# A one-core decoder trunk: the first value unit split in halves, a square moved, the last tile read by column halves, and other schedule offsets

## The chip, the cores and the metric

The kernel runs on one core of one Trainium2 chip. The metric is the device time of one execution in microseconds (us). Times here are from three timed runs of the kernel before and from one profiled execution of it.

## The reference

One decoder block over 512 tokens of 1024 channels, in float32: a mixer of three branches, a merge, and a convolutional feed-forward net.

```python
h = rmsnorm(x); proj = h @ w_in                      # 1024 -> 9216
y_a = (gb * conv3(gc * v)) @ w_a_out                 # short gated convolution
y_b = silu(layernorm(conv31(u * sigmoid(ug)))) @ w_b_out
k, vm = split(rmsnorm(mem) @ w_kv)                   # 256 memory tokens, 4 heads
y_c = softmax(q k^T / 16) vm @ w_att_out
x = x + (sigmoid(g0)*y_a + sigmoid(g1)*y_b + sigmoid(g2)*y_c) @ w_o
u = conv3(rmsnorm(x) @ w_up)                         # 1024 -> 2 * 2816
x = x + (silu(gt) * up) @ w_down
out = rmsnorm(x)
```

## The kernel before, in words

**Products.** TensorE multiplies in float32r. Each operand is split in a high part (ScalarE's cast, `whi` for weights) and a low part (VectorE's subtraction of the high part from the value, `wlo`), and each product is three: high by high, high by low, low by high. A *unit* is a weight tile of 128 x 1024, loaded by one DMA of 512 KB (`wf`, six buffers); its `whi` (L444) and `wlo` (L448) live in a ring of four, so a unit's cast waits until TensorE is through with the unit four places earlier. The large products run in Strassen's manner: a *quad* of four weight blocks u, v, s, r takes seven products, forms 1 to 7, instead of eight (`quad_loads`). The forms 5, 6, 7 and 3 need sums of blocks. These are made mostly by adding DMAs issued on POOL (L582: s5, s6, s7, s3), each of which waits until the low part of the form made before it from the same tile is done. The reads r1 to r7 (`quad_reads`, L651 r1, L655 r5, L658, L666 r6, L672 r4, L401) carry the products' banks into tiles; form 6 goes into the bank that r1 has read.

**Order.** Each step is a *job* with an engine, a cost in us, the jobs that it waits for, and the places (rings of tiles, banks of PSUM) that it takes and uses (`Jobs`). TensorE's jobs have a written order. For all others a list schedule picks, again and again, the job that can start earliest by the planner's costs, and of those with the same start the one due first; a job's due time is counted back from the TensorE product that wants it. `LATER` moves the due times of a kind of job, `AHEAD` keeps a kind from starting more than so many us before its due time. The planner adds 0.2, 0.14 and 0.12 us behind a job of TensorE, ScalarE and VectorE. Every engine then runs its instructions in the order in which the schedule emitted them, SP and POOL among them; a job may emit instructions for an engine other than its own (the final scaling is a VectorE job that also emits a ScalarE copy and the two output DMAs, one on ScalarE's queue).

**The start.** Nine products of the identity (L1697) run while the first loads land. The first unit of the keys, K0, is loaded, cast (L818) and subtracted (L822) in halves of 512 columns, and its products (L871) stand as two jobs; the other units come whole: V(0,0), V(0,1), K(1,0), then the second half of the memory tokens, and so on. The values' products are L395 (high by high), L396 and L397 of `product`. The memory tile's square (`msq`, L734) feeds sums of squares (L750), which TensorE takes after five units.

**The up products.** Their quads are `("up", 0)` to `("up", 10)`; weights beyond the third quad are loaded ahead into free large tiles. The reads need the job `temps`, which opens a new tile pool once the normed rows are transposed. Between w_o and the first forms the normed rows are transposed into banks, of which ScalarE makes high parts (L1598) and plain copies (L1611) and VectorE low parts (L1604).

**The end.** The down product has seven forms a to g, each with two banks, one for each tile t of 128 tokens of a half. The last form, g, does for its units 3 to 5 first t = 0 and then t = 1 (`("pd", "g", "rest")`, 15 products of 512 columns). VectorE adds the bank to the row in `x1` (`read`, L1977; the job `rd`), ScalarE squares the row's half with a sum (L1982, `sq` for the right half, `sr` for the left), VectorE adjusts the right half's sum and multiplies by the gain (`hd`, L1988, L1991), ScalarE takes the root (`rt`, L1996), and `sc` inverts it (L2002), scales both halves (L2003 on ScalarE, L2004 on VectorE) and stores them (L2008).

## Time and profile before

| | us |
|---|---|
| timed, median of 3 (lowest to highest) | 931.41 (930.99 to 931.84) |
| the profiled execution | 931.52 |
| its span, first to last instruction | 929.3 |
| busy: TensorE / VectorE / ScalarE | 916.8 / 837.3 / 672.5 |

A row of the instructions in order of time has the start, the length, the engine (PE is TensorE, PEld its weight load, DVE VectorE, ACT ScalarE, a q behind a name that engine's DMA queue), the line of the kernel, the operation, the output and its inputs, the shape, and in brackets how long the engine had been idle and what ended that. A row of the waits has who waited for whom, and then the total in us, how many times, and the longest. A row of stretches has the stretch, its length, then the busy time of PE, PEld, DVE, ACT and POOL with the number of instructions, TensorE's granted clock, the DMA engines' busy share and GB/s. A row of the DMA view has the transfer, the issuing queue, the count, the size of one and the median time from issue to landing.

### The profile page before, as it was taken

The page shows a single profiled execution, that of the slowest core. Times are in us where ns is not written, and L with a number is a line of the kernel's source. Part 1 is how long each engine was busy: PE and PEld are TensorE (multiplying, and loading weights), DVE is VectorE, ACT ScalarE, POOL GpSimd, SP SyncE. Part 2 cuts the span into 40 slices and gives each one's busy share as a digit, 9 for nine tenths or more (in the row PEclk, how much of TensorE's full clock was granted, in tenths as well). Part 3 has the DMA queues.
Part 4 walks back from the last instruction along what each step waited for, and adds up shares of the span by engine and source line. Part 5 has one row for each costly group of instructions (what it writes and reads, how often), then busy time and mean ns, then how long its engine had stood idle before and what let it go on. Part 6 is the DMA issues. An engine that isn't in the chain of part 4 may idle for free.

```text
span 929.3 us, 16689 instructions
## 1 busy us (share of the span) xinstructions
PE 916.8 (99%) x6644; PEld 860.5 (93%) x6644; DVE 837.3 (90%) x948; ACT 672.5 (72%) x908; POOL 126.5 (14%) x153
## 2 busy tenths in 40 slices
PE   8999999999999999999999999999999999999996
PEld 7999999999989999999899888898999999988885
DVE  6898999969889999999996778897899889999986
ACT  7676988759978879878856743766767676765655
POOL 0121111101111112110100011021211121002300
PEclk9999999999999999999999999999999999999998
DMA  9999678857676799967955598499999878779962
GB/s 356 371 269 236 137 171 178 201 133 136 170 185 170 177 191 243 210 174 183 226 115 158 186 314 179 97 246 295 258 226 235 209 141 166 195 268 329 251 125 91
DMA packets 54077, 190.59 MB, mean 205 GB/s; under 512 B 6128, under 2 KB 6256, under 8 KB 54000
## 3 DMA queue, kind: packets, MB, share of 16 engines
q0 software_dynamic: 20880, 75.24, 45.5%
q1 hardware_dynamic: 32400, 113.23, 34.0%
q8 instruction: 52, 0.85, 0.4%
q10 hardware_dynamic: 720, 1.06, 0.3%
q14 instruction: 25, 0.20, 0.1%
HBM read 185.31 MB, written 4.19 MB: 204 GB/s over the span
## 4 chain that ended last, share of the span: by engine, by line
PE 93%; DMA 3%; ACT 2%; DVE 1%; issue 1%; SPq 0%; ACTq 0%; POOLq 0%
PE bank L624 56%; PE bank L395 6%; PE bank L397 6%; PE bank L396 6%; PE bank L1349 5%; PE bank L1350 5%; PE bank L1351 5%; DMA wf<-in_w_up 2%; PE bank L871 2%; DMA mem<-in_mem_t 1%; ACT whi L444 0%; DVE wlo L448 0%; PE ss L750 0%; PE bank L1098 0%; ACT j L1982 0%
## 5 line engine op out<-in xcount | busy, mean ns | idle before, releaser
L444 ACT CAST whi<-wf 128x1024 fp32r<-128x1024 f32 (+1 forms) x195 | 202.9, 1044 | 100.9 <-PE bank L624 40.1
L448 DVE TENSOR_TENSOR wlo<-wf,whi 128x1024 fp32r<-128x1024 f32 (+1 forms) x189 | 228.3, 1214 | 29.8 <-ACT whi L444 29.4
L1170 ACT ACTIVATE tp<-u,pk 128x510 f32<-128x510 f32 (+22 forms) x184 | 119.7, 706 | 7.5 <-DVE acc L1177 6.5
L1177 DVE TENSOR_TENSOR acc<-acc,tp 128x1022 f32<-128x1022 f32 (+22 forms) x92 | 109.5, 1193 | 4.2 <-ACT tp L1170 2.4
L582 POOL DMA_DIRECT2D wf<-in_w_in x48 | 42.5, 894 | 229.7 <-DVE wlo L448 164.0
L624 PE MATMUL bank<-ft6h,wlo 128*128 128x256 f32 x232 | 64.4, 278 | 1.2 <-DVE wlo L448 1.2
L624 PE MATMUL bank<-ft6h,whi 128*128 128x256 f32 x232 | 64.6, 278 | 1.0 <-ACT gt L651 1.0
L624 PE MATMUL bank<-fb10h,whi 128*128 128x256 f32 x232 | 64.4, 278 | 0.0
L624 PE MATMUL bank<-fb00h,whi 128*128 128x256 f32 x232 | 64.4, 278 | 0.0
L624 PE MATMUL bank<-fb00l,whi 128*128 128x256 f32 x232 | 64.3, 277 | 0.0
L624 PE MATMUL bank<-fb00h,wlo 128*128 128x256 f32 x232 | 64.3, 277 | 0.0
L624 PE MATMUL bank<-ft7h,whi 128*128 128x256 f32 x232 | 64.3, 277 | 0.0
L624 PE MATMUL bank<-ft7l,whi 128*128 128x256 f32 x232 | 64.3, 277 | 0.0
L624 PE MATMUL bank<-ft7h,wlo 128*128 128x256 f32 x232 | 64.3, 277 | 0.0
L624 PE MATMUL bank<-fb11h,whi 128*128 128x256 f32 x232 | 64.3, 277 | 0.0
L624 PE MATMUL bank<-ft5h,wlo 128*128 128x256 f32 x232 | 64.2, 277 | 0.0
L624 PE MATMUL bank<-ft5h,whi 128*128 128x256 f32 x232 | 64.2, 277 | 0.0
L624 PE MATMUL bank<-ft5l,whi 128*128 128x256 f32 x232 | 64.2, 277 | 0.0
L624 PE MATMUL bank<-ft6l,whi 128*128 128x256 f32 x232 | 64.2, 277 | 0.0
L624 PE MATMUL bank<-fb10h,wlo 128*128 128x256 f32 x232 | 64.2, 277 | 0.0
L624 PE MATMUL bank<-fb10l,whi 128*128 128x256 f32 x232 | 64.2, 277 | 0.0
L624 PE MATMUL bank<-fb11l,whi 128*128 128x256 f32 x232 | 64.1, 276 | 0.0
(392 smaller groups left out, 3143.8 us busy)
## 6 DMA issues: line engine op xcount, KB each, us to landing
wf<-in_w_in SPq DMA_DIRECT2D x52, 512.0 KB, 4.9
wf<-in_w_in POOLq DMA_DIRECT2D x48, 512.0 KB, 5.8
wf<-in_w_up SPq DMA_DIRECT2D x29, 512.0 KB, 5.3
wf<-in_w_up POOLq DMA_DIRECT2D x28, 512.0 KB, 6.9
wf<-in_w_down SPq DMA_DIRECT2D x15, 512.0 KB, 4.2
wf<-in_w_v SPq DMA_DIRECT2D x8, 512.0 KB, 10.1
wf<-in_w_att_out SPq DMA_DIRECT2D x8, 512.0 KB, 3.9
wf<-in_w_a_out SPq DMA_DIRECT2D x8, 512.0 KB, 3.8
```

The lines of the kernel that those rows point to most:

```text
L395: nc.tensor.matmul(ps, s_hi, w_hi, start=start, stop=False, skip_group_check=again)
L396: nc.tensor.matmul(ps, s_hi, w_lo, start=False, stop=False, skip_group_check=again)
L397: nc.tensor.matmul(ps, s_lo, w_hi, start=False, stop=stop, skip_group_check=again)
L444: nc.scalar.copy(parts[0], src())
L448: nc.vector.tensor_tensor(lo, src(), hi.bitcast(F32), op=ALU.subtract)
L582: nc.gpsimd.dma_start(out=tiles[key], in_=block(w, col[c], k), accum_op=ALU.add)
L624: nc.tensor.matmul(ps[:, c, :], w[:, k, at], a[k], start=first and n == 0, stop=i == 3 and n == 2, skip_group_check=again,)
L1170: nc.scalar.activation(two(("tp", p, s))[:, j, s:], two(("u", p))[:, j, : SEQ - s], AF.Copy, scale=weight(j),)
L1177: nc.vector.tensor_tensor(a, a, two(("tp", p, s))[:, :, s:], op=ALU.add)
L1349: nc.tensor.matmul(ps, w_hi[:, i, at], hi, start=first, stop=False)
L1350: nc.tensor.matmul(ps, w_hi[:, i, at], lo, start=False, stop=False)
L1351: nc.tensor.matmul(ps, w_lo[:, i, at], hi, start=False, stop=last)
```

## The change

Four things. (1) `halved_unit` makes the loading, casting and subtracting of K0 in halves a helper, and V(0,0) goes through it too: two loads, two casts, two subtractions, and its products as two jobs of six. The square of each memory half now waits for the cast of the unit behind it, V(0,1). Six more products of the identity stand between the two halves of K0's. (2) The last 15 products of 512 columns become 15 of the left 256 columns and 15 of the right 256. VectorE reads the two halves in two jobs, ScalarE squares them in two, and a small VectorE step (`first_end`) joins the left half's sum. (3) The final scaling of token tile 1 waits for the first read of form g. (4) `LATER` and `AHEAD` get other entries.

```diff
 LATER = {
-    "ACT fh h2 t7": 9, "ACT r5 up": -11, "ACT sigmoid": -6, "ACT tp 3": -282, "DVE h t5": 42,
-    "DVE ol": 2, "DVE r2 glu": 48, "DVE tap 2": 21, "DVE vl": 310, "DVE wl up 5": -127,
-    "DVE x1 g": 32, "DVE ymul": 3, "NONE temps": 48.5, "POOL wadd y": -5, "SP ld mix s": -8,
-    "SP ld up v": -78,
+    "ACT r4 cv": 27, "ACT r4 gate": 12, "ACT r4 glu": 5, "ACT r5 glu": 9, "ACT r5 q": 16,
+    "ACT r5 up": 3, "ACT r6 up": -41, "ACT rb": -15.34, "ACT rh": -12, "ACT tp 3": -241,
+    "ACT wh merge 2": -1.66, "ACT wh mix 1": -1, "ACT wh mix 5": 5, "ACT xsquare": 5,
+    "DVE CV": -44, "DVE h t7": 32, "DVE kl": 46, "DVE kt": 33, "DVE ol": 23, "DVE r2 glu": 50,
+    "DVE r2 q": 15, "DVE r3 bb": 16, "DVE rl": 29, "DVE tap 3": 34, "DVE tot1": 160,
+    "DVE vl": 342, "DVE wl K 0": 13, "DVE wl mix 3": -104, "DVE wl mix 5": -5, "DVE wl up 5": -90,
+    "POOL s7 up": -54, "POOL wadd e": 38, "SP ld a 0": 2, "SP ld mix u": 1, "SP ld mix v": -5,
+    "SP ld up r": 9, "SP ld up s": 7, "SP ld up u": -59,
 }
 
 AHEAD = {
-    "ACT fh h2 t7": 10, "ACT sigmoid": 20, "ACT tap 1": 150, "ACT tp 1": 150, "DVE low": 40,
-    "DVE ol": 5, "NONE temps": 40, "POOL wadd y": 10,
+    "ACT r4 gate": 5, "ACT r5 glu": 20, "ACT r5 q": 20, "ACT r5 up": 10, "ACT wh merge 2": 10,
+    "ACT wh mix 1": 5, "ACT wh up 1": 5, "DVE kl": 150, "DVE low": 40, "DVE r2 glu": 5,
+    "DVE r3 bb": 5, "DVE wl mix 5": 5, "POOL wadd e": 40,
 }
...
-        job(("msq", g), "ACT", actv(1024), mem_square, [("ldm", g, 0), ("ldm", g, 1)],
+        job(("msq", g), "ACT", actv(1024), mem_square,
+            [("ldm", g, 0), ("ldm", g, 1), ("wh", ("V", 0, 1))],
...
+    K0, V0 = ("K", 0, 0), ("V", 0, 0)
+
+    def halved_unit(unit, src, n_k):
+        s, raw, parts = unit[0], ("raw", unit), []
+        job(("raw tile", s), "NONE", 0.0, lambda: make(raw), take=[(raw, "wf")])
+        for e in range(2):
+            at = slice(512 * e, 512 * (e + 1))
+            job(("ld0", s, e), "SP", 0.7, lambda at=at: nc.sync.dma_start(
+                out=tiles[raw][:, at], in_=src[:, at]), [("raw tile", s)],
+                LOAD_LATENCY, use=[raw])
...
+                nc.scalar.copy(parts[0][:, at], tiles[raw][:, at])
...
+                nc.vector.tensor_tensor(
+                    lo[:, at], tiles[raw][:, at], hi[:, at].bitcast(F32), op=ALU.subtract
+                )
+
+            job(("wh0", s, e), "ACT", actv(512), high,
+                [("ld0", s, e)] + ([("wh0", s, 0)] if e else []), use=[raw])
+            job(("wl0", s, e), "DVE", dve(512), low, [("wh0", s, e)], use=[raw])
+
+    halved_unit(K0, block(w_kv, 0, 0), 4)
+    halved_unit(V0, w_v[0, 0], 2)
...
+        if (hp, kp) == (0, 0):
+            for e in range(2):
+                pe(V0 if e else ("V0",), 6 * MM, lambda e=e: values_product(0, 0, e),
+                   [("wl0", "V", e)] + lows, take=[] if e else take, use=banks if e else [],
+                   unit=e == 1)
+            return
...
+                if e == 0:
+                    still_warm()
...
+    still_warm = lambda: pe(("warm", 1), 0.7, lambda: warm_up(6), use=[("bank", "warm")], unit=False)
...
+    ENDS = [slice(0, 256), slice(256, 512)]
...
-            pe(("pd", "g", "rest"), 5 * 3 * MM, lambda: steps("g", (3, 4, 5), (1,)),
-               use=banks + [(s, p, g) for s in ("zh", "zl") for g in (1, 2)], unit=False)
+            for i, cols in enumerate(ENDS):
+                pe(("pd", "g", "rest", i), 15 * MM_QUAD,
+                   lambda cols=cols: steps("g", (3, 4, 5), (1,), cols),
+                   use=banks + [(s, p, g) for s in ("zh", "zl") for g in (1, 2)], unit=False)
...
+    def first_end():
+
+        ss = ss_fin[NT - 1][:, 1:2]
+        nc.vector.scalar_tensor_tensor(ss, ss_end, 1.0 / D, ss, op0=ALU.mult, op1=ALU.add)
...
+                for i, end in enumerate(ENDS):
+                    job(("rd", p, t, i), "DVE", dve(256), lambda end=end: read("g", 1, end),
+                        [("pd", "g", "rest", i)] + rows_in, use=[("bank", chain(p), t)])
...
+            job(("sr", t, 0), "ACT", 0.4, lambda: square(last, 0, ENDS[0], ss_end),
+                [("rd", "g", 1, 0)])
+            job("ends", "DVE", 0.1, first_end, [("sr", t, 0), ("hd", t)])
+            job(("sr", t, 1), "ACT", 0.4, lambda: square(last, 0, ENDS[1]), [("rd", "g", 1, 1)])
+            ready = [("sr", t, 1), "ends"]
+        job(("rt", t), "ACT", 0.3, lambda t=t: root(t), ready)
+        job(("sc", t), "DVE", 0.95, lambda t=t: scaled(t),
+            [("rt", t)] + ([("rd", "g", 0)] if t == 1 else []))
```

More of the change, by code (lines that the diff above doesn't have):

```diff
@@ L829, in hybrid_block_kernel, with high, low @@
-    first_parts = []
+    K0, V0 = ("K", 0, 0), ("V", 0, 0)
[7 more added lines that the diff above has]
+                LOAD_LATENCY, use=[raw])
+            def high(e=e, at=at):
+                if e == 0:
+                    parts.extend(
+                        wts.tile([P, 1024], F32R, tag=s, name=name(s)) for s in ("whi", "wlo"))
+                    w_units[unit] = [t.rearrange("p (k n) -> p k n", k=n_k) for t in parts]
+                nc.scalar.copy(parts[0][:, at], tiles[raw][:, at])
+            def low(at=at):
+                hi, lo = parts
+                nc.vector.tensor_tensor(
[4 more added lines that the diff above has]
+            job(("wl0", s, e), "DVE", dve(512), low, [("wh0", s, e)], use=[raw])
@@ L1692, in hybrid_block_kernel, with warm_up @@
     NU = len(PAIR_UNITS)
[L1693 to L1696 removed]
+    def warm_up(n):
+        ps = tiles["bank", "warm"]
+        for i in range(n):
             nc.tensor.matmul(ps[:, :P], ident, ident, start=True, stop=True)
[L1699 removed]
+    pe(("warm",), 4.9, lambda: (make(("bank", "warm")), warm_up(9)),
+       take=[(("bank", "warm"), "ps")], unit=False)
+    still_warm = lambda: pe(("warm", 1), 0.7, lambda: warm_up(6), use=[("bank", "warm")], unit=False)
     KEYS = lambda h, g: lambda: pe_keys(h, g)
```

101 lines of the change are left out of this document (43 added, 58 removed).

## The prediction

> **What bounds the kernel now.** I read the page first, then who waited for whom on TensorE, then a table by stretches, and then the instructions in order of time at the places these name.
>
> ```profile
> span 929.3 us, 16689 instructions
> PE 916.8 (99%) x6644; PEld 860.5 (93%) x6644; DVE 837.3 (90%) x948; ACT 672.5 (72%) x908; POOL 126.5 (14%) x153
> ```
> ```profile
> PE bank L624 <- DVE wlo L448: 1.2, 2, 0.8
> PE bank L624 <- ACT gt L651: 1.0, 2, 0.8
> PE bank L396 <- DVE wlo L448: 0.8, 1, 0.8
> PE bank L871 <- ACT whi L818: 0.5, 1, 0.5
> PE bank L871 <- DVE wlo L822: 0.2, 1, 0.2
> ```
> ```profile
> 600.00:700.00 100.00, 97.76 (x842) 96.76 (x841) 88.37 (x101) 70.33 (x93) 19.04 (x22) 1.00 0.98 251
> ```
>
> TensorE is the bound: 916.8 of 929.3 us. The second fence has all its waits on another engine but the very first (total, times, longest): 3.7 us. The third shows that 2.24 of them lie between 600 and 700 (the second number is TensorE's busy time); the rest is in the first 12 us, and after the last product, at 921.5, only the output's tail of some 7 us is left. The diff changes no product's count of multiplied columns, so the time can fall only by these waits and by the tail. That caps the gain at some 6 us of 931 however good the new schedule is; nothing caps a loss, since VectorE is busy 90%.
>
> The profiled execution took 931.52 us with its span of 929.3, so 2.2 lie around the span; the three timed runs have a median of 931.41, 0.1 below. I work against 931.5.
>
> **Part 1: the start.**
>
> ```profile
> 7.17 0.28 PE L871 MATMUL bank<-mh,wlo 128*128 128x256 f32 x1
> 7.93 0.38 PE L871 MATMUL bank<-mh,whi 128*128 128x256 f32 x1 [0.48 <-ACT whi L818]
> ```
> ```profile
> 9.91 0.41 PE L395 MATMUL bank<-whi,mh 128*128 128x512 f32 x1
> 11.09 0.50 PE L396 MATMUL bank<-wlo,mh 128*128 128x512 f32 x1 [0.77 <-DVE wlo L448]
> 11.43 0.39 PE L397 MATMUL bank<-whi,ml 128*128 128x512 f32 x1
> ```
> ```profile
> 7.27 0.60 ACT L818 CAST whi<-wf 128x512 fp32r<-128x512 f32 x1
> 7.78 1.05 ACT L734 ACTIVATE msq<-mem 128x1024 f32<-128x1024 f32 x1
> 8.74 1.03 ACT L444 CAST whi<-wf 128x1024 fp32r<-128x1024 f32 x1
> ```
> ```profile
> 7.91 0.69 DVE L822 TENSOR_TENSOR wlo<-wf,whi 128x512 fp32r<-128x512 f32 x1
> ```
>
> The values' first unit has its high part at 9.8 and waits for its low part, so its second product (L396) starts at 11.09 where 9.91 + 0.23 was due (products of 512 columns start 0.227 apart when nothing waits). With the 0.11 of the next step TensorE loses 1.06 us.
>
> After the change ScalarE goes from the keys' second half (7.27) straight to two halves of 0.60 (L818's row), at 7.78 and 8.34. The unit's load lands 5.7 us after its issue:
>
> ```profile
> 2.59 0.91 SPq L474 DMA_DIRECT2D wf<-in_w_v x2
> ```
> ```profile
> wf<-in_w_v SPq DMA_DIRECT2D x1, 512.0 KB, 5.7
> ```
> That is 8.3, and half of it sooner, by how much no row shows: I take 7.7. VectorE's two halves of 0.69 follow its own at 7.91: done at 9.2 and 9.75 (and at 9.6 and 10.2 if both came at 8.3, still ahead of TensorE). The next unit, V(0,1), issued right behind, lands at about 9.6 and is cast to about 10.65; the memory's square (1.05) now comes behind that, to about 11.7, and the cast of K(1,0), which ended at 8.74 + 3 x 1.03 or so = 11.9, ends near 12.7. Its low part is then there at about 13.9, and TensorE wants it at 15.6. The square's reader, the squares' sum, is wanted by TensorE at 22 only. So the move costs nothing; without that slack it would be the 0.8 by which ScalarE runs later from 12 on. One more DMA issue on SP costs nothing: loads land here 5.7 us after their issue, behind others. If that cover were gone, the later loads would slip by the issue's own time.
>
> The six warm-up products stand between the halves of the keys. The nine at the start are 18 rows, so six are 12. Their price is not seen at this place:
>
> ```profile
> 1.36 4.21 PE L1697 MATMUL bank<-ident 128*128 128x128 f32 x18 [1.36 <-POOL ident masks.py:199]
> ```
> ```profile
> 22.09 1.68 PE ss L750 x16
> ```
>
> The same form at the start gives 4.21/18 = 0.23 a row, the nearest float32 products afterwards 1.68/16 = 0.105: 12 rows are 1.26 to 2.8 us. The keys' products run 0.114 apart (256 columns) at 7.2 as they do later, so I take 0.105: 7.17 + 0.11 + 1.26 = 8.54, where the keys' second half started at 7.93 but had its low part only at 8.6 (7.91 + 0.69). Its twelve products end at about 10.0 where they ended at 9.91: the filling costs 0.1, and 1.6 at the dear end. From 10.0 the values run unbroken to 12.7; before, their twelfth ended its slot at 13.7 (11.43 + 10 x 0.227). **Start: -0.95 us** (ends +0.6 and -1.05). What is late next: the unit after it needs its low part at 12.9, and has it at about 11.9; K(0,1), behind it, is wanted from 18.2, and with 0.8 more on ScalarE should still be there some tenths before; squares, scale rows and x's norm follow TensorE, and their vector work moves along.
>
> **Part 2: the last token tile.**
>
> ```profile
> 921.53 0.39 PE L397 MATMUL bank<-whi,zl 128*128 128x512 f32 x1
> ```
> ```profile
> 921.82 0.16 DVE L2002 RECIPROCAL cols<-cols 128x1 f32<-128x1 f32 x1 [1.12 <-ACT cols L1996]
> 922.02 0.75 DVE L2004 SCALAR_TENSOR_TENSOR x<-x,cols,gfin 128x512 f32<-128x512 f32 x1
> 922.69 0.68 DVE L1977 TENSOR_TENSOR x<-x,bank 128x512 f32<-128x512 f32 x1
> ```
> ```profile
> 923.41 0.63 ACT L1982 ACTIVATE j<-x 128x512 f32<-128x512 f32 x1 [0.66 <-DVE x L1977]
> ```
> ```profile
> 925.44 0.37 ACTq L2008 DMA_DIRECT2D out<-x  x1
> ```
> ```profile
> 599.31 1.09 ACT L1611 COPY h2b<-bank 128x512 f32<-128x512 f32 x2
> ```
> ```profile
> 599.94 0.69 DVE L1604 TENSOR_TENSOR fb00l<-bank,fb00h 128x512 fp32r<-128x512 f32 x1 [0.20 <-ACT h2b L1611]
> ```
>
> The last product starts at 921.53 and ends by the profile 0.39 later; with a hand-over VectorE can read at 921.96. It reads at 922.69, as token tile 2's scaling (922.02) is ahead of it. From there to the output's issue at 925.44 are 2.75 us. TensorE's 30 products of 256 columns take what 15 of 512 took.
>
> *Best end.* The first half is read while TensorE does the second, the second at 921.96, and nothing stands in between: 0.73 earlier, a read shorter by 256/960 = 0.27, a square shorter by 256/1200 = 0.21. That is -1.2.
>
> *What I take.* The read at 599.94 waits for a ScalarE copy that only reads the same bank; it needs nothing of it. So the program keeps two engines apart by the whole bank, and the first half's read, emitted after the second half's products, waits for them too. And the list schedule emits by earliest start, with its own costs: counted from the first half's start, the read of the other tile at 0.20-0.81, its square and root to 2.06, the first half's read at 1.91, tile 2's scaling at 2.25, the half square at 2.37, the join of the sums at 3.20, the last read at 3.63. On VectorE the first read, waiting to 921.96, then holds up tile 2's scaling, whose copy and DMA issue hold up the half square on ScalarE, which holds up the join, which holds up the last read: 921.96 + 0.34 (half read) + 0.20 (921.82 to 922.02) + 0.75 (as 922.02) + 0.42 (the issue's 0.37 and a hand-over) = 923.67; half square 0.63 - 0.21 and 0.1 for its sum, 0.52; join and hand-over 0.2; last read at 924.39, then 2.75 less the 0.48 that the halves save: 926.66. **Tail: +1.2 us** (ends -1.2 and +1.2; tile 1's scaling now waits for the other tile's read: that only swaps the two on VectorE, which then idles 1.12 before 921.82; without that idle time it would cost the read's 0.68).
>
> The Trainium skill's page "PSUM — Partial Sum Buffer", under "PSUM bank collisions raise a hardware error", says to guard by bank and quadrant, not by address, disjoint columns included; by that rule the halves cannot overlap. The rows at 599 agree, with 0.20 us of wait.
>
> **Part 3: the schedule.**
>
> ```profile
> 622.75 0.39 PE L624 MATMUL bank<-ft6h,whi 128*128 128x256 f32 x1 [0.23 <-ACT gt L651]
> ...
> 637.77 0.39 PE L624 MATMUL bank<-ft6h,wlo 128*128 128x256 f32 x1 [0.76 <-DVE wlo L448]
> ...
> 646.81 0.38 PE L624 MATMUL bank<-ft6h,whi 128*128 128x256 f32 x1 [0.82 <-ACT gt L651]
> ```
> ```profile
> 621.63 0.58 ACT L655 COPY uu<-bank 128x512 f32<-128x512 f32 x1
> 622.11 0.59 ACT L651 COPY gt<-bank 128x512 f32<-128x512 f32 x1
> ```
> ```profile
> 635.41 1.05 ACT L444 CAST whi<-wf 128x1024 fp32r<-128x1024 f32 x1 [2.62 <-DMA wf<-in_w_up]
> ```
> ```profile
> wf<-in_w_up POOLq DMA_DIRECT2D x1, 512.0 KB, 12.1
> ```
> ```profile
> wf<-in_w_up POOLq DMA_DIRECT2D x1, 512.0 KB, 6.0
> ```
>
> Idle are 0.23, 0.76 and 0.82 us, and 0.43 of the 2.24 remain for a fourth wait, just behind the third. Each also hides 0.17 under its predecessor's row (0.28 long, 0.11 apart) and is followed by a step that is 0.11 late: 0.5, 1.0, and 1.1 + 0.7, in all 2.24 + 4 x 0.28 = 3.4. The first waits for read r1 (L651), which stood behind r5 (L655, 0.48): r5 of the up quads goes from 11 earlier to 3 later, so this 0.5 should go. The second waits for a weight that came by an adding DMA of 12.1 us; the one before took 6.0 at a quieter time. It shared the queues with loads of later quads. Their order changes (v no longer 78 earlier, u 59 earlier, the seventh form's add 54 earlier); landing a few microseconds sooner, it removes the 1.0, and the third wait's chain, which hangs behind it, comes as much earlier, for 1.0 of the 1.1. **Schedule: -2.5 us** (0.5 + 1.0 + 1.0); ends -3.4 and, as every other offset can also make a wait where there is none now, +5.6 (below). Elsewhere I cost the offsets at nothing: between 11.5 and 622 TensorE waits for nothing, under VectorE's 90%, and that cover is thin.
>
> **Sum:** 931.5 - 0.95 + 1.2 - 2.5 = **929.2 us** (929.25).
>
> **Rivals.**
> - *The halves do overlap* and the tail gains its 1.2, with the rest as forecast: 931.5 - 0.95 - 1.2 - 2.5 = 926.8. For it: only the 599.94 row speaks of banks, and it is one row. Against: that row, and the order on two engines. 12%.
> - *The stalls move but do not shrink*, because the adding DMAs are slow from the sum of the traffic (DMA share 0.98 from 600 to 700), not from its order; start and tail cancel: 931.5 - 0.95 + 1.2 = 931.7. 20%.
> - *A loss: the early u loads delay an adding DMA that has no slack.* One that takes 12.1 in place of 6.0 is 6.1 late. The sixth form of the first up quad is cast at 620.67, and that row too ends a wait on its DMA:
>
> ```profile
> 620.67 1.05 ACT L444 CAST whi<-wf 128x1024 fp32r<-128x1024 f32 x1 [1.85 <-DMA wf<-in_w_up]
> ```
>
>   TensorE wants it at 622.2 and its low part 0.2 later: the rival decides from a slip of about 0.5 us on. A full slip costs 6.1 less the 0.5 stall there now: 5.6, and 931.7 + 5.6 = 937.3; half of it gives 934.5. 30%.
>
> **Numbers.** The forecast has 38%, with 928 to 929.5 as its own range. Faster by over 0.2% (below 929.55) are it and the overlap: 0.50. Within 0.2%, which is about what a measurement of this kernel can tell from no change: 0.20. Slower: 0.30. The range runs from 926.2, just under the overlap, to 934.6, half a slip; beyond it lie some 17% above and 3% below.
>
> **What would show it.** Start: the values' second product 0.23 after the first, and the next unit at 12.7. If the twelve warm-up rows are 0.2 apart, the keys' second half starts near 10 and the gain is gone. Tail: VectorE's first half read starting only about 0.4 after the last product's start, and the output's last issue over 4.5 us after that product; if the read starts some 1.7 us earlier the halves overlap and my tail is wrong. Schedule: L651 before L655 for the first up quad, adding DMAs near 6 us, TensorE's waits between 600 and 660 at about 1 us. A TensorE wait of over 2 us anywhere after 60 us makes the prediction wrong.

## The result and the profile after

The changed kernel took **936.85 us** (median of 6 runs, 935.17 to 940.38) beside 931.62 for the kernel before on the same chip (6 runs, 930.99 to 933.26): a ratio of 1.0058, 95% interval 1.0041 to 1.0074. It is slower by 0.6%, clear of the interval. The forecast of 929.2 and the range up to 934.6 were wrong; the rival with the loss had named 934.5 to 937.3. The profiled execution took 937.16, with a span of 935.4 us, beside 931.52 and 929.3 before.

The page of the changed kernel and its list of TensorE's waits (total, times, longest):

```profile
span 935.4 us, 16730 instructions
PE 920.4 (98%) x6671; PEld 864.8 (92%) x6671; DVE 836.9 (89%) x951; ACT 674.2 (72%) x914; POOL 127.0 (14%) x153
```
```profile
PE bank L629 <- ACT whi L449: 2.2, 1, 2.2
PE bank L629 <- ACT pr L1038: 1.9, 1, 1.9
PE bank L1721 <- POOL ident masks.py:199: 1.4, 1, 1.4
PE bank L629 <- DVE wlo L453: 0.8, 1, 0.8
```

The small waits of before are gone; two of about 2 us have come, where the prediction allowed none. (Each kernel has line numbers of its own: L624 of before is L629 here, L444 is L449, L651 is L656, and the experiments shift them again.)

To see where the time went, the same product is looked up in both traces, and its two starts are subtracted:

| product | before | after | later by |
|---|---|---|---|
| first of the unit behind the first values | 16.47 | 15.55 | -0.92 |
| behind the transposes of the first two heads | 180.11 | 181.64 | +1.53 |
| first on the merged g | 594.34 | 596.52 | +2.18 |
| sixth form of the first up quad | 622.75 | 624.50 | +1.75 |
| fourth form of the first up quad | 633.75 | 640.79 | +7.04 |
| its later forms | 650.37 | 654.75 | +4.38 |
| last product of all | 921.53 | 926.34 | +4.81 |
| issue of the last output | 925.44 | 931.24 | +5.80 |

Read by steps: start -0.9; +2.4 to 181 us, of which 2.2 are one stall at 179; +0.7 around 428 to 436; the first named wait -0.4; stalls at 633 to 641 us +5.3; the waits behind it -2.7; +0.4 to the last product's start, 0.3 of it in the halved products (they start 0.120 apart, where 0.113 is half of the 0.227 before); the tail +1.0. A wait of TensorE costs 0.28 more than the idle time in the brackets, since it begins under the row before it and the first step behind it is 0.11 late: 1.90 is 2.2 in all, 2.16 is 2.4, 0.76 is 1.0.

*The start.* In the instructions in order of time (start, length) the values' second product now follows the first by 0.23, as forecast:

```profile
9.95 0.40 PE L400 MATMUL bank<-whi,mh 128*128 128x512 f32 x1
10.18 0.40 PE L401 MATMUL bank<-wlo,mh 128*128 128x512 f32 x1
```

*The stall at 179 us.* ScalarE's instructions there (L1038 is the exp of the scores, L1159 the conv sigmoid, L1194 the conv products), the product of TensorE that waited, with the idle time before it in brackets, and last the first exp of the second head in the kernel before:

```profile
171.05 1.28 ACT L1038 ACT_TABLE_LOAD   x1 [1.03 <-DVE cols L1032]
...
173.39 1.28 ACT L1159 ACT_TABLE_LOAD   x1
174.68 1.06 ACT L1159 ACTIVATE ug<-ug 128x1024 f32<-128x1024 f32 x1
175.75 1.28 ACT L1038 ACT_TABLE_LOAD   x1
...
179.37 1.30 ACT L1194 ACTIVATE tp<-u,pk 128x487 f32<-128x487 f32 x2
180.57 0.47 ACT L1038 ACTIVATE pr<-bank,cols 128x256 f32<-128x256 f32 x1
```
```profile
181.64 0.39 PE L629 MATMUL bank<-fb10h,whi 128*128 128x256 f32 x1 [1.90 <-ACT pr L1038]
```
```profile
177.57 0.48 ACT L1014 ACTIVATE pr<-bank,cols 128x256 f32<-128x256 f32 x1 [2.24 <-DVE cols L1008]
```

A sigmoid between two exps costs not 1.06 but 3.6 us, as the table is loaded before it and again behind it. That is more than the 2.24 us that ScalarE stood idle here before, and a pair of conv products takes another 1.2. The sigmoid stands there because the new list lets the conv quads' second read (r2) come only 5 us ahead of its due time: the four sigmoids began at 86.1 to 143.1 us before, and at 104.2 to 174.7 us now; in e5 below, which lacks that one entry, they begin at 85.3 to 142.3 and the wait is gone.

*The stalls at 633 us.* POOL's instructions, each the issue of one adding DMA (the row of 623.48 holds two, at 623.48 and 624.02); then the DMA view of the issue at 623.48 alone and of both issues (KB, median us from issue to landing); then ScalarE's cast and TensorE's products that waited; and last, from the kernel before, POOL's issue of the same two and the time of the first:

```profile
614.41 0.86 POOL L587 DMA_DIRECT2D wf<-in_w_up  x1 [1.97 <-DMA wf<-in_w_up]
623.48 1.76 POOL L587 DMA_DIRECT2D wf<-in_w_up  x2 [8.21 <-DMA wf<-in_w_up]
626.41 0.86 POOL L587 DMA_DIRECT2D wf<-in_w_up  x1 [1.18 <-DVE wlo L453]
```
```profile
wf<-in_w_up POOLq DMA_DIRECT2D x1, 512.0 KB, 5.3
wf<-in_w_up POOLq DMA_DIRECT2D x2, 512.0 KB, 7.7
```
```profile
634.20 2.94 ACT L449 CAST whi<-wf 128x1024 fp32r<-128x1024 f32 x3 [5.05 <-DMA wf<-in_w_up]
```
```profile
635.30 0.39 PE L629 MATMUL bank<-fb11h,whi 128*128 128x256 f32 x1 [2.16 <-ACT whi L449]
636.56 0.39 PE L629 MATMUL bank<-fb11h,wlo 128*128 128x256 f32 x1 [0.76 <-DVE wlo L453]
```
```profile
619.13 0.86 POOL L582 DMA_DIRECT2D wf<-in_w_up  x1 [7.07 <-DVE wlo L448]
621.29 0.86 POOL L582 DMA_DIRECT2D wf<-in_w_up  x1 [1.30 <-DMA wf<-in_w_up]
```
```profile
wf<-in_w_up POOLq DMA_DIRECT2D x1, 512.0 KB, 5.9
```

The issue at 623.48 is s5 of the third up quad, which idled POOL for 8.21 us until its own load had landed. Behind it, in order, stood s3 of the first quad, whose tile had been free from about 621.0. It went out at 624.02 and took 2 x 7.7 - 5.3 = 10.1 us, while before it went out at 619.13, ahead of s5, and took 5.9. So the third form's weight came at 634.2, and TensorE had wanted it at 633.

Behind these waits TensorE itself is slow. Three stretches of 3.41 us each; TensorE's busy time with the number of products stands behind the length, and the granted clock behind that:

```profile
633.77:637.18 3.41, 1.12 (x7) 1.00 1.03 308
637.18:640.59 3.41, 3.41 (x19) 0.50 1.03 419
640.59:644.00 3.41, 3.41 (x31) 1.00 1.04 407
```

*The tail.* The last product starts at 926.34. Then, of VectorE and ScalarE:

```profile
926.65 0.42 DVE L2010 TENSOR_TENSOR x<-x,bank 128x256 f32<-128x256 f32 x1 [2.04 <-PE bank L402]
...
927.18 0.72 ACT L2044 ACTIVATE x<-x,cols 128x512 f32<-128x512 f32 x1 [1.35 <-DVE cols L2043]
...
928.35 0.42 ACT L2016 ACTIVATE j<-x 128x256 f32<-128x256 f32 x1 [0.45 <-ACT x L2044]
...
928.89 0.16 DVE L2034 SCALAR_TENSOR_TENSOR cols<-cols 128x1 f32<-128x1 f32 x1 [0.96 <-ACT j L2016]
928.97 0.42 DVE L2010 TENSOR_TENSOR x<-x,bank 128x256 f32<-128x256 f32 x1
```

The first half's read waited 2.04 us for the second half's products, and the second read stood behind the join, which stood behind the third tile's scaling: 4.90 us to the last issue, where there were 3.91.

### The profile page after: what moved, and what is told of

Same layout as the page of the kernel before. It is cut to its first block, busy times and chain, and to the rows that moved or that the text cites. A ratio compares the mean times of both kernels' runs of the same rounds, so it can differ in the third digit from the quotient of the medians.

```text
span 935.4 us, 16730 instructions
## 1 busy us (share of the span) xinstructions
PE 920.4 (98%) x6671; PEld 864.8 (92%) x6671; DVE 836.9 (89%) x951; ACT 674.2 (72%) x914; POOL 127.0 (14%) x153
## 3 DMA queue, kind: packets, MB, share of 16 engines
q10 hardware_dynamic: 720, 1.06, 0.3%
## 4 chain that ended last, share of the span: by engine, by line
PE 95%; DMA 2%; ACT 1%; DVE 1%; issue 0%; POOL 0%; ACTq 0%; POOLq 0%; DVEq 0%
PE bank L629 57%; PE bank L400 7%; PE bank L402 7%; PE bank L401 7%; PE bank L1373 5%; PE bank L1375 5%; PE bank L1374 5%; PE bank L883 2%; DMA wf<-in_w_up 2%; PE bank L1721 1%; DVE wlo L453 0%; PE ss L756 0%; ACT whi L449 0%; PE bank L1122 0%; ACT pr L1038 0%; PE bank L1610 0%
## 5 line engine op out<-in xcount | busy, mean ns | idle before, releaser
L449 ACT CAST whi<-wf 128x1024 fp32r<-128x1024 f32 (+1 forms) x201 | 209.1, 1044 | 104.3 <-PE bank L629 44.9
L453 DVE TENSOR_TENSOR wlo<-wf,whi 128x1024 fp32r<-128x1024 f32 (+1 forms) x195 | 235.2, 1212 | 36.5 <-ACT whi L449 36.1
L1194 ACT ACTIVATE tp<-u,pk 128x506 f32<-128x506 f32 (+22 forms) x184 | 119.2, 706 | 4.3 <-DVE acc L1201 2.3
L1201 DVE TENSOR_TENSOR acc<-acc,tp 128x966 f32<-128x966 f32 (+22 forms) x92 | 109.1, 1188 | 4.0 <-ACT tp L1194 2.5
L587 POOL DMA_DIRECT2D wf<-in_w_in x52 | 46.2, 911 | 266.3 <-DVE wlo L453 201.5
L629 PE MATMUL bank<-fb11h,whi 128*128 128x256 f32 x232 | 65.2, 281 | 2.2 <-ACT whi L449 2.2
L629 PE MATMUL bank<-fb10h,whi 128*128 128x256 f32 x232 | 64.4, 278 | 1.9 <-ACT pr L1038 1.9
L629 PE MATMUL bank<-fb11h,wlo 128*128 128x256 f32 x232 | 64.9, 280 | 0.8 <-DVE wlo L453 0.8
L629 PE MATMUL bank<-fb11l,whi 128*128 128x256 f32 x232 | 64.8, 279 | 0.0
L629 PE MATMUL bank<-ft7h,whi 128*128 128x256 f32 x232 | 64.5, 278 | 0.0
L629 PE MATMUL bank<-fb00h,whi 128*128 128x256 f32 x232 | 64.4, 278 | 0.0
L629 PE MATMUL bank<-ft6h,whi 128*128 128x256 f32 x232 | 64.4, 277 | 0.0
L629 PE MATMUL bank<-ft7l,whi 128*128 128x256 f32 x232 | 64.4, 277 | 0.0
L629 PE MATMUL bank<-ft7h,wlo 128*128 128x256 f32 x232 | 64.4, 277 | 0.0
L629 PE MATMUL bank<-fb00l,whi 128*128 128x256 f32 x232 | 64.3, 277 | 0.0
L629 PE MATMUL bank<-fb00h,wlo 128*128 128x256 f32 x232 | 64.3, 277 | 0.0
L629 PE MATMUL bank<-ft5h,wlo 128*128 128x256 f32 x232 | 64.3, 277 | 0.0
L629 PE MATMUL bank<-ft5h,whi 128*128 128x256 f32 x232 | 64.3, 277 | 0.0
L629 PE MATMUL bank<-ft5l,whi 128*128 128x256 f32 x232 | 64.3, 277 | 0.0
L629 PE MATMUL bank<-ft6h,wlo 128*128 128x256 f32 x232 | 64.2, 277 | 0.0
L629 PE MATMUL bank<-ft6l,whi 128*128 128x256 f32 x232 | 64.2, 277 | 0.0
L629 PE MATMUL bank<-fb10h,wlo 128*128 128x256 f32 x232 | 64.2, 277 | 0.0
```

What stands on the lines that cost most here:

```text
L449: nc.scalar.copy(parts[0], src())
L453: nc.vector.tensor_tensor(lo, src(), hi.bitcast(F32), op=ALU.subtract)
L587: nc.gpsimd.dma_start(out=tiles[key], in_=block(w, col[c], k), accum_op=ALU.add)
L629: nc.tensor.matmul(ps[:, c, :], w[:, k, at], a[k], start=first and n == 0, stop=i == 3 and n == 2, skip_group_check=again,)
L1194: nc.scalar.activation(two(("tp", p, s))[:, j, s:], two(("u", p))[:, j, : SEQ - s], AF.Copy, scale=weight(j),)
L1201: nc.vector.tensor_tensor(a, a, two(("tp", p, s))[:, :, s:], op=ALU.add)
```

## The experiments

Theory A: the loss is made at the two stalls and in the tail, by the order in which the new lists put a few instructions into in-order queues. Against it stood that the new start makes the stalls (B), that tail and clock are the loss (C), that waits would stay or only move (D, F, H), that what is gained is given back at a transfer which ends at a time of its own (E), that the slow products are not from idleness (G), and that halves cost by being halves (J). The traces of d1, d3, e3, e8, f2 and f3 are of the fastest execution of their run, that of d2 of the slowest, so a trace and its run's median can tell different sizes; where they do, both are given. Each run has the kernel before timed on the same chip beside it (930.4 to 931.0 us); on that scale the changed kernel is about 936.1.

### Lists alone, edits alone

e1: all code edits, the old LATER and AHEAD. e2: the old code, the new LATER and AHEAD. e3: of the edits only the start, old lists. e4: of the edits only the tail, old lists.

> The changed kernel with the two lists of offsets of the kernel before: the code edits alone. Theory A (the lists make the loss, the code edits nearly cancel): -0.92 us at the start and +1.0 us in the tail, so 931.7 us beside 931.6 of the kernel before, and no TensorE wait over 2 us between 170 and 660 us. Rival B (the earlier start of TensorE, 0.92 us ahead of the same transfers, makes the stalls, whatever the lists): the two waits of about 2 us at 179 and 633 us stay and the time is 934.5 to 937 us. Rival C (the loss is the tail and a lower clock): 934 us or more with no wait over 2 us.

> The kernel before with the two new lists of offsets: the lists alone. Theory A: the wait at 179 us (2.4 us) and those at 633 us (2.5 + 2.8 us with the slow products behind them) are there, the three waits of before behind 620 us (0.4 + 2.7 us) are gone, and 936.8 us comes out beside 931.6. Rival B (only lists and earlier start together make the stalls): 928.5 to 931.5 us, as forecast for the schedule. Rival C (tail and clock): 931 to 932 us.

> The kernel before with the halved value unit, the moved square and the second warm filling alone, old lists, old tail. Theory A: TensorE is 0.92 us ahead from 16 us to the end, as the trace of the changed kernel has it to 178 us, and 930.7 us comes out beside 931.6. Rival B (the lead is lost at the next transfer that has no slack): 931.6 us or more, with a new wait where the lead is lost; if the earlier start makes the stalls at 179 and 633 us, 934 us or more.

> The kernel before with the last token tile by halves of its columns alone, old lists, old start. Theory A: from the last product to the issue of the last output 4.9 us in place of 3.9, and up to 0.4 us in the halved products ahead of it: 932.6 us (932.4 to 933.0) beside 931.6. Rival (the tail costs nothing by itself, and the changed kernel's 1.0 us comes from the clock or from the lists): 931.4 to 931.9 us.

| run | us | beside 930.75: ratio, 95% interval |
|---|---|---|
| e1 | 931.98 | 1.0014, 1.0005 to 1.0022 |
| e2 | 938.37 | 1.0075, 1.0057 to 1.0094 |
| e3 | 930.22 | 0.9996, 0.9988 to 1.0005 |
| e4 | 932.66 | 1.0021, 1.0012 to 1.0030 |

The lists make the loss: with the old code they have the 2.2 us wait at 180 and a wait of 5.0 at 633. B and C fall. The tail alone costs 1.9 us (0.2%), at the forecast's size beside 930.75 (1.0 to 1.4) or a little over it; e4's trace shows 1.0 in the tail and 0.3 in the halved products. With it e1 stands 1.2 us above the kernel before where 0.1 was expected. The start alone was to give 0.92 and gives 0.5, with zero inside the interval. The trace of e4, whose start is the old one, says why. From it, two of the first products; then the landing of the keys' second half, issued at 2.12, in the kernel before and in e4; and ScalarE's high part of the memory tokens' second half, which stands ahead of that half's cast, in the same two:

```profile
8.98 0.50 PE L395 MATMUL bank<-whi,mh 128*128 128x512 f32 x1
10.24 0.50 PE L396 MATMUL bank<-wlo,mh 128*128 128x512 f32 x1 [0.76 <-DVE wlo L448]
```
```profile
wf<-in_w_kv SPq DMA_DIRECT2D x1, 256.0 KB, 5.0
```
```profile
wf<-in_w_kv SPq DMA_DIRECT2D x1, 256.0 KB, 4.0
```
```profile
6.46 0.91 ACT L714 ACTIVATE mh<-mem,pk 128x256 fp32r<-128x256 f32 x2 [1.27 <-DMA mem<-in_mem_t]
```
```profile
5.49 0.91 ACT L714 ACTIVATE mh<-mem,pk 128x256 fp32r<-128x256 f32 x2 [0.25 <-DMA mem<-in_mem_t]
```

In the execution that the prediction was made against, both loads happened to land 1.0 us later than in e4. e4 has the old wait and still begins the next unit at 15.62, where the profile of before had 16.47 and the changed kernel has 15.55. Over all traces the old start reaches it at 15.62, 16.23 and 16.47, the new one at 15.45 to 16.15 (15 traces). The reason is the filling: with the loads on time, the keys' second half follows the first at once in e4 and the values begin at 8.98, while the twelve warm-up rows hold them back to 9.9 or later in every trace of the new start. So the filling gives back what the split saves (1.06), unless a load is late.

### One list entry taken back

```diff
 AHEAD (e5, e7)
-    "DVE r2 glu": 5,
 LATER (e6, e7)
-    "SP ld up r": 9,
```

> The changed kernel without one entry of its second list, the 5 us by which the second reads of the conv quads (r2) may come ahead of their due time. Beside a kernel before of 930.75 us the changed kernel stands at 936.1 (ratio 1.0058). Theory A: the four sigmoids go back to about 83, 103, 123 and 142 us, the two extra table loads between the exps at 171 to 176 us go, TensorE's 2.2 us wait at 179 us goes, the waits at 633 to 636 us stay: 933.7 us (933.3 to 934.2). Rival D (the exps wait for the scores anyway, and the wait stays or moves to the next head): 935.5 to 936.5 us. Rival E (the 2.4 us are given back at 633 us, because the adding transfer there ends at a time of its own): 935.8 us, with a wait of 4.5 us or more at 633.

> The changed kernel without one entry of its first list, the 9 us on the loads of the up quads' r tiles; in the planner this alone puts the adding DMA s3 of the first up quad ahead of s5 of the third on the POOL queue again. Theory A: the waits of 2.4 and 1.0 us at 633 to 636 us go, and with them the 15 slow products behind (1.5 us): 931.2 us, or up to 933.0 where a part of the 2.7 us of waits at 637 and 646 us of the kernel before comes back; the wait at 179 us stays. Rival F (POOL's order is not it, the transfer itself is late): 935.5 to 936.5 us with the wait still there.

> The changed kernel without both entries. Theory A: the two gains add, 928.8 us (928.3 to 930.5), below the kernel before. Rival E (gains at 179 us are given back at 622 to 647 us by transfers that end at a time of their own): 930.5 to 932 us, with waits of 0.5 to 1.2 us there as in the kernel before.

Measured: e5 943.55 (1.0125, 1.0104 to 1.0147), e6 940.46 (1.0098, 1.0083 to 1.0113), e7 943.05 (1.0124, 1.0107 to 1.0141), all worse than the change. Locally each did what A said: in e5 TensorE is 2.3 us ahead at 181 and 2.4 at 217; in e6 the stalls at 633 are gone, 5.0 us. e6 has s3 ahead of s5 on POOL, so the entry `SP ld up r` had turned the two round. Then a new wait comes, in e5 (first fence) at 427 and in e6 (second) at 651, and e7 has one at each place (425 and 655):

```profile
426.95 0.58 PE L616 MATMUL bank<-ft6h,whi 128*128 128x256 f32 x1 [5.99 <-ACT g L643]
```
```profile
PE bank L616 <- ACT whi L436: 4.4, 1, 4.4
```

The planner decides every later instruction by what it decided before; one entry taken back re-sorts the queues for hundreds of microseconds. Such a run does not undo one part of a list, it makes another schedule. So the next edits keep the plan and move single instructions in it.

### Products in the idle time

```diff
+        for _ in range(2 if (q, f) == (("up", 1), 2) else 1):
             for c in range(2):
```

> The changed kernel, in which the second form of the second up quad, the last products ahead of the wait at 633 us but for one form, is multiplied twice into the same bank (24 more products of 0.107 us, 2.6 us, started anew the second time); schedule and lists as changed. Theory A with the clock: TensorE's 2.4 us of idleness are filled, the 15 products behind at 0.213 us run at 0.107, and the time is 934.6 us (936.1 less 1.5, and less 0.0 to 0.3). Rival G (the slow products come from something other than the idle time, a shared load on the chip or the late weights): they stay, and the time is 936.1 to 936.5 us.

Measured: 937.86 (1.0070, 1.0050 to 1.0090), no gain in time; the profiled execution took 935.48. The doubled form stands six forms ahead of the third one, at 612 to 618 us, so it does not fill the idle time; it brings TensorE to the third form 2.8 us later. In e8's trace the waits at 633 are gone, and no product behind them is slow. 630 to 650 us in the changed kernel, then in e8:

```profile
630.00:650.00 20.00, 17.08 (x132) 0.91 1.04 325
```
```profile
630.00:650.00 20.00, 18.94 (x165) 1.00 1.04 323
```

So the slow products belong to the idleness and not to a load on the chip, against G: the DMA engines are as busy in both. Nor are they bound to late weights: in e5 and e7 the clock fell as well behind waits for another reader (L643, above). The price of the clock is the 1.6 us that these 15 products at 0.213 take over 0.107. As a remedy it fails in the runs' median (the trace is of the fastest of four, 935.48 to 939.63), presumably because the transfer lands later in other executions; that was not traced.

### The plan kept, single instructions moved

The planner runs as in the changed kernel; its calls are collected, and before they are made the named ones are moved. The traces show that SP and POOL do keep their order but for the named moves; on VectorE and ScalarE some neighbours are swapped from build to build, also between the changed kernel and e8, whose lists are the same. One such swap matters, in the tail (see f3). In d3 the planner also gets the old tail:

```diff
-            fn()
+            todo.append((key, fn))
...
+        for key, by, other in MOVES:
...
+MOVES d1: s5 of ("up", 2) behind s3 of ("up", 0)
+MOVES d2: ("sg", 3), ("tp", 0, 25) behind ("exp", 1, 1)
+MOVES d3: both, with the old tail and "sc 1" behind "rd g 0"
```

> The changed kernel with its plan kept whole (every queue in the order as planned, every buffer in its place) but for one instruction: the adding DMA s5 of the third up quad is issued on POOL behind s3 of the first one, not ahead of it. Theory A (s3 waits on POOL's queue for a transfer that itself waits for its load): s3 is issued near 621 us, lands by 627 to 628, the waits of 2.4 and 1.0 us at 633 and the slow products behind them go, 5.3 us in all; up to 1.8 us come back at 646 to 651 us, where s5 and its successors land a little later: 931 to 932.7 us beside 936.1 of the changed kernel. Rival F (moving it only moves the wait, as the removal of one offset did at 651 us): 935 to 940 us with a wait over 3 us at 646 to 651.

> The changed kernel with its plan kept whole but for two instructions: the last conv sigmoid and one pair of conv products are issued on ACT behind the four exps of the first two heads, not between them. Theory A: two table loads fewer ahead of the second head's exps, the wait of 2.2 us at 179 us goes, and nothing else is moved, so no new wait at 425 us: 933.8 us (933.3 to 934.3). Rival E (the 2.3 us come back at 633 us, where the adding DMA ends at a time of its own): 935.5 to 936.5 us with a wait of 4.5 us or more there.

> The changed start and the new lists with both of these moves, the tail of the kernel before (whole columns), and the second tile's scale behind the first read of g. Theory A: 936.1 less 2.3 (wait at 179), less 5.3 and plus up to 1.8 (633 to 651), less 1.0 to 1.4 (tail), less up to 0.5: 927.5 to 929.5 us, below the kernel before at 930.8. Rival E (the transfers of 620 to 650 us end at times of their own, so that what is gained ahead of them is given back there): 930 to 931.5 us, with waits of 2 us or more in all between 620 and 652.

| run | us | beside 930.37: ratio, 95% interval |
|---|---|---|
| d1 | 934.01 | 1.0033, 1.0021 to 1.0045 |
| d2 | 937.76 | 1.0075, 1.0061 to 1.0089 |
| d3 | 933.67 | 1.0035, 1.0022 to 1.0048 |

**d1 settles the larger stall.** POOL's two issues, and the landing time of the first, in d1:

```profile
620.71 0.86 POOL L599 DMA_DIRECT2D wf<-in_w_up  x1 [6.13 <-DVE wlo L465]
622.83 0.86 POOL L599 DMA_DIRECT2D wf<-in_w_up  x1 [1.25 <-DMA wf<-in_w_up]
```
```profile
wf<-in_w_up POOLq DMA_DIRECT2D x1, 512.0 KB, 5.6
```

s3 lands at 626.3 in place of 634.2, and s5 lands at 629.3 in place of 628.8, since it waited for its load anyway. From 436 to 641 us TensorE gains 5.0, and 0.9 comes back at 647. Against F no wait is over 1.1. But the median gains only 2.3 (1.0058 to 1.0033), and 934.01 lies above the 931 to 932.7 that A gave; the trace is of the fastest of the five, and 0.7 of its gain is the tail's swap. What the others lost was not traced.

**d2 missed.** The wait at 179 went, but ScalarE's next reads came late: new waits of 1.1 at 182 and 1.5 at 217, and TensorE was 0.8 later than in the changed kernel by 218. And at 633 it waited longer (d2's trace), 4.1 where it had been 2.2, as s3's transfer took 11.9:

```profile
637.81 0.58 PE L642 MATMUL bank<-fb11h,whi 128*128 128x256 f32 x1 [4.05 <-ACT whi L462]
```

Behind the exps ScalarE has no room for the sigmoid either. d3 has d2's loss in it, and misses for that: at 655 us it is 2.8 us ahead of the changed kernel, where f1 below is 6.1 ahead.

### The sigmoid early, the tail in another order, and all three

```diff
+MOVES f2: ("r2", ("glu", 3)) behind ("r3", ("glu", 3)); ("sg", 3) behind that
+MOVES f3: ("sc", 2) ahead of ("rd", "g", 1, 0); "ends" behind ("rd", "g", 1, 1)
+MOVES f1: those of d1, f2 and f3
+MOVES f4: all edits, old lists; f3's, and ("r1", ("up", 0)) ahead of ("r5", ("up", 0))
+MOVES f5: as f1, with ("sg", 3) ahead of the cast of (("q", 0), 3)
```

> The changed kernel with its plan kept whole but for three places: s5 of the third up quad behind s3 of the first on POOL; the last conv gate's read and its sigmoid ahead, at about 141 us, out of the attention stretch; in the tail the third tile's scale ahead of the two half reads and the join behind them. Theory A (three separate places, each loss undone where it arises): 936.1 less 2.3 (181 us), less 5.5 and plus 1.2 (633 to 651), less 1.6 (tail): 928.0 us (927.3 to 929.3), below the kernel before at 930.5. Rival E (transfers end at times of their own): what is gained at 181 us is given back at 622 to 651 us, 930 to 931.5 us.

> The changed kernel with its plan kept whole but for the last conv gate's read on DVE and its sigmoid on ACT, moved ahead to about 141 us. Theory A (the table loads and the sigmoid cost only because they stand in the attention stretch, where ACT sets the pace): the 2.2 us at 179 us go, no wait comes at 182 or 217 us, and TensorE is 2.3 us ahead from 181 to 600 us: 933.8 us (933.0 to 935.0, the wait at 633 us varies). Rival H (ACT has no room anywhere from 100 to 217 us): waits of 1 us or more between 140 and 217 us and 935.5 to 937 us.

> The changed kernel with its plan kept whole but for the tail's order of emission: the third tile's scale ahead of the first half read, the join behind the second. Theory A (the halves lose by standing in the wrong order in two in-order queues, not by being halves): from the last product to the issue of the last output 3.3 us in place of 4.9, 934.5 us. Rival J (the halves pay twice for fixed costs, and the bank lets neither half be read before the last product): 4.2 us or more, 935.5 us or more.

> All code edits of the changed kernel with the old lists (the run at 932.0 beside 930.75), its plan kept whole but for the same order of the tail, and the first up quad's first read ahead of its fifth on ACT. Theory A: 1.6 us less in the tail and 0.5 us less at 622 us: 929.9 us beside 930.75 (929.3 to 930.5). Rival J: the tail gives 0.7 us at most, 931 to 931.6 us.

> The run with three moves, its sigmoid now issued behind the read of the first query quad, where ACT stood idle for 1.2 us at 147 us. Theory A: the wait of 0.9 us at 145 us goes, nothing comes in its place, and the time is 929.2 us (928.7 to 929.8) beside 930.84 of the kernel before, below it by more than the interval. Rival H (ACT has no room between 100 and 217 us): a wait of 0.5 us or more moves to 148 to 156 us and the time stays at 929.8 to 930.5 us.

| run | us | kernel before | ratio, 95% interval |
|---|---|---|---|
| f1 | 930.03 | 930.84 | 0.9993, 0.9984 to 1.0002 |
| f2 | 937.62 | 930.84 | 1.0077, 1.0064 to 1.0091 |
| f3 | 934.13 | 930.84 | 1.0036, 1.0022 to 1.0050 |
| f4 | 930.76 | 930.84 | 1.0000, 0.9991 to 1.0008 |
| f5 | 929.38 | 930.35 | 0.9990, 0.9981 to 1.0000 |

**f2** has TensorE 1.6 us ahead at 181 (2.3 less a wait of 0.9 at 145, where the sigmoid now stands before a read), and its median is no better than the change, as E said. But E's mechanism is not in its trace, of the fastest of five (933.96): there s3 goes out 2.6 earlier and lands 3.4 earlier, the wait at 633 is shorter, and TensorE is 3.3 ahead of the changed kernel at 655. Why the other executions lose the lead stays open. In f1, with s3 ahead of s5, the lead is kept to the end in the trace. f1 is 6.1 us ahead of the changed kernel at 655. Its median of 930.03 lies in the range that E had named, where A said 928.0: A's sum took the profiled execution's sizes and left out the 0.9 at 145. **f5** moves the sigmoid to where ScalarE was idle; the wait at 145 goes, TensorE is 2.4 ahead at 181, and none of its waits is over 1.3 us but the very first, which every trace has:

```profile
PE bank L1737 <- POOL ident masks.py:199: 1.4, 1, 1.4
PE bank L645 <- ACT gt L672: 1.3, 1, 1.3
PE bank L645 <- ACT g L687: 0.6, 1, 0.6
```

Its 0.6 at 427 is new. At 0.10% under the kernel before, f5 is the fastest of all; its 929.38 is in A's range, but A wanted it below the kernel before by more than the interval, and the interval just touches 1.

So three moves of single instructions take the changed kernel from 0.58% above the kernel before to 0.07% below it: the two stalls and the tail's order are the loss.

**f3**: the same halves in another order. Its last product starts at 924.60; the rows are the two reads, the first square and the last issue:

```profile
925.00 0.74 DVE L2023 TENSOR_TENSOR x<-x,bank 128x256 f32<-128x256 f32 x2
...
925.50 0.42 ACT L2029 ACTIVATE j<-x 128x256 f32<-128x256 f32 x1 [0.45 <-DVE x L2023]
...
927.72 0.37 ACTq L2062 DMA_DIRECT2D out<-x  x1
```

3.12 us to the last issue, in place of 4.90 and of 3.91 before. d1 and e1 show one half of it by chance: there the join happens to stand behind the second read, and the tail takes 4.22. So the join's place is worth 0.7 and the third tile's scaling 1.1. A holds against J: the halves lost by order. But neither half is read before the last product, and e3, with whole columns, happens to end in 3.18 us too, as its planner put the second tile's root ahead of the first one's scaling on ScalarE, which brought the third tile's scaling out of the last read's way. So the halves give nothing that the order alone does not, and cost 0.2 to 0.3 as products.

**f4** missed by 0.9. Its tail took 3.11, but at 622 us the lead of the start was lost again. ScalarE there:

```profile
621.37 1.05 ACT L458 CAST whi<-wf 128x1024 fp32r<-128x1024 f32 x1 [3.40 <-DMA wf<-in_w_up]
622.33 0.58 ACT L665 COPY gt<-bank 128x512 f32<-128x512 f32 x1
```

r1 (L665) is ahead of r5 now and is still late: both stand behind a cast that waits for its DMA. From the cast's start to the sixth form's first product are 1.59 us here and 2.08 in the kernel before, so the swap gave the 0.5 that it was priced at; but the cast began 0.70 later. In the changed kernel, and in f1 and f5, r1 stands far ahead of the cast. ScalarE's r1 and cast in f5, and TensorE's product, which does not wait:

```profile
612.76 1.09 ACT L672 COPY gt<-bank 128x512 f32<-128x512 f32 x2
...
621.23 1.05 ACT L465 CAST whi<-wf 128x1024 fp32r<-128x1024 f32 x1 [0.79 <-DMA wf<-in_w_up]
```
```profile
622.48 0.28 PE L645 MATMUL bank<-ft6h,whi 128*128 128x256 f32 x1
```

## Why the prediction was wrong

- **The failed step is the schedule, -2.5 us, in its sentence "Elsewhere I cost the offsets at nothing".** The offsets made 2.2 us at 179 and 5.3 at 633 (3.4 of waits, the rest a slower clock behind them). d1 and f2/f5 show both places by moving one and two instructions. The argument had been that TensorE waited for nothing there; that says how it stood in the old order, not how much a new order has to spare. The rows of ScalarE around the exps, and of POOL around 615 to 625 with their idle times, were there to be read against the new entries.
- **The waits that it did count** are gone from the changed kernel's trace, for 0.4 + 2.7 = 3.1 us, but the 2.7 partly by luck: TensorE came 7 us later to that place. With the stalls repaired (d1, f1, f5) the second wait and the one behind the third stay away, and the third is there again with 1.1 to 1.6 us. So the third did not hang behind the second, as the prediction had it, and from the first products of 619 us to 650 us these traces gain 1.0 to 1.6 on the kernel before, not 2.5.
- **The loss rival was right in kind and price, wrong in place.** It put a late adding DMA at up to 6.1 us and 937.3. The transfer was late by 9.2 at landing (634.2 against 625.0 before), but it was s3 for the third form, held up by POOL's order, and not an effect of the early u loads on the sixth form. No rival named the conv sigmoids.
- **The first wait** went because r1 moved ahead of the cast that waits for its DMA. The prediction's r5 before r1 was a part of it, with the 0.5 that it had priced; in f4 that part alone did not help.
- **The start** came out as worked, -0.92 of -0.95, against its own execution, and that was luck in part. The filling was taken at 0.1, because the keys' second half was late in that execution; its twelve rows took 1.26 us (7.19 to 8.45), and with the loads on time, as in e4, old and new start reach the next unit at 15.62 and 15.55. As a difference of medians the start gives 0.5 with zero in the interval. A lead from it also meets a transfer at 622: e1 and f4 have lost all of it by there, while e3 has its lead again by 640.
- **The tail** was right: +1.0 of +1.2 in the same trace, by the steps named, the bank-wide wait and the order of emission. "TensorE's 30 products of 256 columns take what 15 of 512 took" was 0.2 too low (3.6 against 3.4). The tail's best end, with the halves overlapping, was not reached by any run.
- **Small items:** the moved square cost nothing that the traces show. The +0.7 at 428 to 436 is no part of the change's price by itself: e8, with the same order there, is 0.8 earlier at that place.

## What to carry to other kernels

Where a program places instructions by list offsets, cost a changed offset by the queue that it re-sorts: for every in-order queue write down what stands behind each moved instruction, what that instruction itself waits for, and when the next reader wants it. "TensorE does not wait here now" is not slack. And to test one cause in such a kernel, freeze the order and move one instruction; changing the offset back makes a third schedule. And go by the medians for the size: here a lead ahead of a late transfer (f2) was worth nothing in the median, and was kept once that transfer was early (f1).

## What the runs showed of the hardware

The granted clock fell to 0.50 behind some stalls and not behind others. It fell after waits of 1.1 and 1.0 us with 0.2 between (f3), of 1.6 and 1.0 (f2), of 2.4 and 1.0 (the changed kernel), and of 3.7 to 6.3 (d2, e2, e5, e6, e7); not after one wait of 2.2 (at 179), nor after 1.1 and 0.7 with 0.2 between (before). In the clock records of these traces each of the ten slow stretches lasted 3.41 or 6.83 us, and each began a whole number of 3.41 us behind the first reading of full clock; so the clock is set for fixed stretches of 3.41, and where a wait falls in them matters. The Trainium skill, on the page "TensorE: Matmul & The Clock Gate", in its Part 1 on the clock gate, gives half rate as the state after at least one idle window of about 3.4 us, a window that runs freely. The half rate (0.213 beside 0.107 us) and the window's length agree; but 2.1 us of waiting in all were enough here (f3), in two pieces inside one such length, so a window need not be wholly idle. How much of it must be idle the runs do not settle, since the one wait of 2.2 inside a window did not do it.

The same adding DMA of 512 KB, s3, took 5.6 us when issued at 620.7 (d1) and 10.1 when issued at 624.0, behind another of its kind: 3.3 us of delay on the queue became 7.9 at the landing. In the seven traces in which s3 goes 0.5 us behind s5 it took 8.8 to 12.1 us, in the eleven in which it goes ahead 5.5 to 8.7. Of these, the four with the old lists (e1, e3, e4, f4) took 6.0 to 8.7 and the other seven 5.5 to 5.9; what makes that difference was not traced.
